# Attention heads' small products in other slots of a hand-planned decoder block, and ALiBi slopes moved into two scales

## The chip, the cores and the metric

One NeuronCore of a Trainium2 chip runs the whole program. The metric is the device time of one execution in microseconds; it was 438.44 us, the median of three runs (438.3 to 439.01). TensorE (PE) multiplies matrices, VectorE (DVE), ScalarE (ACT) and GpSimd (POOL) work on elements, SyncE (SP) issues most transfers. Each engine executes its instructions in the order in which the program writes them.

## The reference

One decoder block on 256 tokens of width 1024 in float32. With n = rmsnorm(x):

```
cu, cg, q, k, v, gc, ga = split(n @ w_in)
y_conv = silu(layernorm(causal_conv31(cu * sigmoid(cg)) + dw_b)) @ w_conv_out
att    = per head: softmax(rms(q) rms(k)^T / sqrt(128) - slope_h * distance, causal) @ v
merged = sigmoid(gc) * y_conv + sigmoid(ga) * (att @ w_attn_out)
h      = x + merged @ w_out
out    = h + (silu(r @ w_gate) * (r @ w_up)) @ w_down,   r = rmsnorm(h)
```

There are 8 heads of width 128, and slope_h = 2^-(h+1). All 256 tokens lie in one attention block, so no past block is selected and the attention is an ordinary causal one with a linear bias.

## The kernel before

**Main stream.** The weights come in pieces of 512 KB, one for each *slot*. For each piece ScalarE rounds it to a high part `whi` (line 154), VectorE (or GpSimd for some odd pieces between 12 and 60) subtracts it for the low part `wlo` (line 155), both six slots ahead of their use, and PE makes products in three terms, high by high, high by low, low by high (`mm3`, lines 173 to 175). A slot of the first 80 has 12 products of 512 columns, six for tokens 0 to 127 and six for tokens 128 to 255. The order of the slots is fixed: convolution inputs 0 to 15; q, k, v of heads 0 to 3 in 16 to 27; q, k, v of heads 4 to 7 in 28 to 39; gates 40 to 55; attention output (`ao`) 56 to 63; convolution output (`co`) 64 to 71; `wo` 72 to 79; then gate and up (`gu`), then down (`dn`).

**Small work beside it.** The rest is put into slots by four lists: `pre[slot]` stands ahead of the slot's first six products, `jobs[slot]` between the first six and the last six, `post[slot]` behind the last six, `late[slot]` after these. `busy` counts jobs of a slot.

**A head** (`head`) turns its q and k into columns (`turn`, line 429, tile `tq`), multiplies them (`score`, lines 439 and 440, tile `sc`), adds distances that ScalarE has scaled by the head's slope (line 437) and takes the row's extreme on VectorE (`most`), exponentiates two slots later, divides one slot after that, transposes the probabilities four slots after the score (`turn_p`, line 465, tile `tp`) and multiplies them with the values one slot later (`values`, lines 473 and 474, tile `pv`). All of these write one of two PSUM banks of tag `tr`.

**The convolution** runs as 31 taps for each of 8 channel groups on VectorE (line 273), two groups ("channels" here) at a time. `refill` (line 261, tile `cv`) transposes the next two groups into PSUM. `norm_stats` (line 336, tile `ytr`) transposes the finished pair back, and after the last pair layernorm's scale is made and `norm_back` (line 359, tile `yb`) makes silu on ScalarE (line 363), its high part `yh` (line 365) and its low part `yl` (line 366), the operands of `co`.

**The planner.** `run_taps` puts taps behind a slot as long as an estimated sum of VectorE's work, `load["dve"]`, stays below that of PE's, `load["pe"]`, plus 1.0. Each slot adds 2.6 (`SLOT`) to PE's sum and 1.14 (`LOW_PART`) to VectorE's unless GpSimd makes the low part; a tap adds 0.4 (0.53 when one channel alone is left); `pe_side` and `dve_side` add what small work costs in its slot; VectorE's sum is never below PE's less 2.6. So in which slot a tap, a refill, the statistics and `norm_back` stand follows from these sums. A pair's refill comes two slots after its predecessor's end, its statistics three or more, and `norm_back` two and three slots after the last statistics.

Of the kernel before, what the change touches and what calls it, by code (L numbers as in the profile page):

```python
# [9 lines left out]
F32 = mybir.dt.float32  # L10
F32R = mybir.dt.float32r
BF16 = mybir.dt.bfloat16
AF = mybir.ActivationFunctionType
# [3 lines left out]
P = 128  # L17
# [3 lines left out]
H = 8  # L21
# [4 lines left out]
CW = 512  # L26
G = 2
EPS = 1e-6
U = G * CW // P
SHIFT = 48  # L30
BIG = 1e30
# [3 lines left out]
C_QG = 4 * KD  # L35
# [7 lines left out]
SPL_BUFS = 8  # L43
AHEAD = 6

HEAD_STEP = ((0, 3, 6, 9), (0, 3, 5, 7))

SLOT = 2.6
LOW_PART = 1.14
# [3 lines left out]
REFILL = 2  # L53
# [34 lines left out]
def hybrid_block(ctx: ExitStack, tc: tile.TileContext, x, xT, par, w_in, w_co, w_ao, w_o, w_gu, w_dn, out):  # L88
    nc = tc.nc

    cst = ctx.enter_context(tc.tile_pool(name="cst", bufs=1))
# [13 lines left out]
    pre, jobs, post, late = (defaultdict(list) for _ in range(4))  # L105
    busy = defaultdict(int)
# [128 lines left out]
    rstd = cst.tile([P, T], F32, name="rstd")  # L235
    rhalf = cst.tile([P, T], F32, name="rhalf")
    rstd2 = cst.tile([P, T], F32, name="rstd2")
    gqs = cst.tile([P, 1], F32, name="gqs")

    def r1(t):  # L240
        return rstd[:, t : t + 1]
# [15 lines left out]
    def refill(ch):  # L257

        j, cv = ch["next"], ch["cv"]
        for t in range(T):  # L260
            nc.tensor.transpose(cv[:, KC - 1 + t * P : KC - 1 + (t + 1) * P],
                                ca[j // 2][:, t, (j % 2) * P : (j % 2 + 1) * P], ident)
        cacc[j] = ea.tile([P, S], F32, tag="cacc", bufs=4, name=f"cacc{j}")
        ch["j"], ch["k"], ch["next"] = j, 0, j + 2
# [11 lines left out]
    def run_taps(slot, until):  # L276
        while load["dve"] + TAP <= until:
            live = [ch for ch in chains if ch["j"] is not None]
            if not live:
                return  # L280
            load["turn"] += 1
            ch = live[load["turn"] % len(live)]
            conv_tap(ch)
            load["dve"] += TAP if len(live) > 1 else TAP_ALONE
            if ch["k"] == KC:
                j, ch["j"] = ch["j"], None
                want_refill(slot, ch)
                if j % 2:
                    last = j == KD - 1
                    at_ = slot + 3  # L290
                    while not last and busy[at_] > 1:
                        at_ += 1
                    busy[at_] += 1
                    jobs[at_].append(lambda p=j // 2: norm_stats(p))
                    pe_side[at_] += 0.45
                    dve_side[at_] += 0.7
                    if last:
                        for i in range(4):
                            jobs[at_ + 2 + i // 2].append(lambda i=i: norm_back(2 * i))

    def want_refill(slot, ch):
        j = ch["next"]
        if j < KD and j // 2 in ca:
            clear(ch)
            slot += REFILL
            post[slot].append(lambda: refill(ch))
            pe_side[slot] += 0.25
            dve_side[slot] += 0.1

# [20 lines left out]
    def norm_stats(p):  # L330
        if not yt:
            yt[0] = ea.tile([P, T, D], F32, tag="yt", name="yt")
        tr = bank(f"ytr{p}", T, 256)
        for t in range(T):
            for j in range(2):
                nc.tensor.transpose(tr[:, t, j * P : (j + 1) * P], cacc[2 * p + j][:, t * P : (t + 1) * P], ident)
        nc.scalar.copy(yt[0][:, :, p * 256 : (p + 1) * 256], tr)
        for t in range(T):
            nc.vector.bn_stats(bst[:, t, p, :], tr[:, t, :])
        if p == KD // 2 - 1:  # L340
            norm_scale()
# [64 lines left out]
    def v_done(b):  # L406
        def done(slot, acc):
            def evac(t):
                if not vs:
                    vs[0] = ea.tile([P, T, D], F32, tag="vs", name="vs")  # L410
                nc.scalar.activation(vs[0][:, t, b * CW : (b + 1) * CW], acc[t], AF.Copy, scale=r1(t))

            late[slot + 1].append(lambda: evac(0))
            late[slot + 2].append(lambda: evac(1))
            for i in range(4):
                head(slot + 1 + i, slot + 2 + HEAD_STEP[b][i], 4 * b + i)
        return done

    def head(first, slot, h):
        hs = slice((h % 4) * P, (h % 4 + 1) * P)  # L420
        vh = slice(h * P, (h + 1) * P)
        halves = ((0, slice(0, 1)), (1, slice(1, 3)))
        s = {}

        def turn():
            tq = bank(f"tq{h}", 4, P)
            for i, n in enumerate("qk"):
                for t in range(T):
                    nc.tensor.transpose(tq[:, 2 * i + t, :], qk[n, h // 4][:, t, hs], ident)
            s["q"] = sm.tile([P, S], F32, tag="qT", bufs=4, name=f"qT{h}")  # L430
            s["k"] = sm.tile([P, S], F32, tag="kT", bufs=4, name=f"kT{h}")
            nc.scalar.activation(s["q"], tq[:, 0:2, :], AF.Copy, scale=gqs)
            nc.scalar.activation(s["k"], tq[:, 2:4, :], AF.Copy, scale=prm[:, C_KG : C_KG + 1])

        def score():
            s["bias"] = sm.tile([P, 3, P], F32, tag="bias", name=f"bias{h}")
            nc.scalar.mul(s["bias"], dist, 2.0 ** (-8.0 * (h + 1) / H))
            s["sc"] = bank(f"sc{h}", 4, P)
            nc.tensor.matmul(s["sc"][:, 1:3, :], s["q"][:, P:], s["k"], start=True, stop=True)
            nc.tensor.matmul(s["sc"][:, 0, :], s["q"][:, :P], s["k"][:, :P], start=True, stop=True)  # L440
            most()

        def most():
            s["nmx"] = sm.tile([P, T], F32, tag="nmx", name=f"nmx{h}")
            for t, b in halves:
                nc.vector.tensor_tensor_reduce(s["bias"][:, b, :], s["sc"][:, b, :], s["bias"][:, b, :], scale=-1.0,
                                               scalar=3.0e38, op0=ALU.add, op1=ALU.min,
                                               accum_out=s["nmx"][:, t : t + 1])

        def expo():  # L450
            p = s["p"] = sm.tile([P, 3, P], F32, tag="p", name=f"p{h}")
            den = s["den"] = sm.tile([P, T], F32, tag="den", name=f"den{h}")
            for t, b in halves:
                nc.scalar.activation(p[:, b, :], s["bias"][:, b, :], AF.Exp, bias=s["nmx"][:, t : t + 1], scale=-1.0,
                                     accum_out=den[:, t : t + 1])
            nc.gpsimd.tensor_tensor(den, den, mone, op=ALU.pow)

        def divide():
            for t, b in halves:
                nc.scalar.activation(s["p"][:, b, :], s["p"][:, b, :], AF.Copy, scale=s["den"][:, t : t + 1])  # L460

        def turn_p():
            tp = bank(f"tp{h}", 4, P)
            for i in range(3):
                nc.tensor.transpose(tp[:, i, :], s["p"][:, i, :], ident)
            s["pT"] = sm.tile([P, 3, P], F32, tag="pT", name=f"pT{h}")
            nc.scalar.copy(s["pT"], tp[:, 0:3, :])

        def values():
            if not aoT:  # L470
                aoT[0] = pair("ao")
            pv = bank(f"pv{h}", S)
            nc.tensor.matmul(pv, vs[0][:, 0, vh], s["pT"][:, 0:2, :], start=True, stop=False)
            nc.tensor.matmul(pv[:, P:], vs[0][:, 1, vh], s["pT"][:, 2, :], start=False, stop=True)
            nc.scalar.copy(aoT[0][0][:, h, :], pv)
            nc.vector.tensor_sub(aoT[0][1][:, h, :], pv, aoT[0][0][:, h, :].bitcast(F32))

        for i in (first, slot, slot + 4, slot + 5):
            busy[i] += 1
        pe_side[first] += 0.45  # L480
        pe_side[slot] += 0.65
        pe_side[slot + 4] += 0.35
        pe_side[slot + 5] += 0.65
        dve_side[slot] += 0.7
        dve_side[slot + 5] += 0.35
        jobs[first].append(turn)
        jobs[slot].append(score)
        pre[slot + 2].append(expo)
        pre[slot + 3].append(divide)
        jobs[slot + 4].append(turn_p)  # L490
        jobs[slot + 5].append(values)


    sgs = ea.tile([P, 2, T, D], F32, tag="sgs", name="sgs")
# [229 lines left out]
    def first_norm():  # L724
        ss = bank("ss", T)
        for t in range(T):
            nc.tensor.matmul(ss[:, t : t + 1], sq[:, 0, t * P : (t + 1) * P], ones, start=True, stop=True)
        nc.vector.tensor_scalar(rstd, ss, 1.0 / D, EPS, op0=ALU.mult, op1=ALU.add)
        nc.gpsimd.tensor_tensor(rstd, rstd, mhalf[:, :T], op=ALU.pow)
        nc.gpsimd.tensor_scalar_mul(rhalf, rstd, 0.5)  # L730
        nc.gpsimd.tensor_scalar_mul(gqs, prm[:, C_QG : C_QG + 1], float(P) ** -0.5)

    post[4].append(first_norm)
    late[0].append(lambda: nc.scalar.dma_start(prm, par))
# [108 lines left out]
```

## Time and profile before

| | |
|---|---|
| median of three runs | 438.44 us (438.3 to 439.01) |
| the profiled execution | 437.82 us, span 436.0 us |
| TensorE clock granted | 0.999 of full speed |
| PE busy | 431.2 us, 99% of the span |
| VectorE, ScalarE, GpSimd busy | 314.8, 248.1, 87.3 us (72, 57, 20%) |
| transfers | 80.30 MB, 184 GB/s on average |

The profile is of one execution. PE's busy time counts pipelined products with modelled ends, so the distances between their starts say more than the share. A slot can be found in the trace by counting 12 products of the main stream.

### The profile page before, as it was taken

To read this page: it belongs to the slowest core of one execution; us is meant where nothing else is said; L and a number is where in the kernel's file an instruction comes from. 1 tells how busy PE (TensorE), PEld (TensorE's weight loads), DVE (VectorE), ACT (ScalarE), POOL (GpSimd) and SP (SyncE) were. 2 spreads that over 40 slices of the span, in tenths; PEclk is the share of its full clock that TensorE was granted. 3 is DMA by queue.
4 is the path that set the end of the run, shared out by engine and by line. 5 is a ranking of instruction groups with operands and counts; after the bars stand their busy time and mean duration, and the time that the engine had idled before them with its cause. 6 is when DMAs were issued, how large, how long until landed. Compare 5 with 4: busy or idle time off the path is not lost.

```text
span 436.0 us, 6861 instructions
## 1 busy us (share of the span) xinstructions
PE 431.2 (99%) x2514; PEld 376.4 (86%) x2514; DVE 314.8 (72%) x558; ACT 248.1 (57%) x451; POOL 87.3 (20%) x74
## 2 busy tenths in 40 slices
PE   8999999999999999999999999999999999999997
PEld 5788888888888888888888899999999999888886
DVE  4989999898889799967678368666666666644501
ACT  6765456789998676639435276455444555533300
POOL 1624465644572534200000000000000000000000
PEclk9999999999999999999999999999999999999999
DMA  8986665355445444654936536555555555775001
GB/s 277 337 284 224 230 260 186 132 194 209 144 142 165 153 138 144 194 177 149 309 122 190 188 106 232 168 192 193 194 196 196 190 196 193 247 228 201 37 0 50
DMA packets 23202, 80.30 MB, mean 184 GB/s; under 512 B 2560, under 2 KB 2944, under 8 KB 23168
## 3 DMA queue, kind: packets, MB, share of 16 engines
q1 hardware_dynamic: 22752, 78.66, 53.5%
q10 hardware_dynamic: 416, 1.19, 0.8%
q8 instruction: 20, 0.33, 0.3%
q14 instruction: 14, 0.11, 0.1%
HBM read 78.80 MB, written 1.05 MB: 183 GB/s over the span
## 4 chain that ended last, share of the span: by engine, by line
PE 95%; ACT 1%; DMA 1%; DVE 1%; SPq 1%; issue 0%
PE gu L191 9%; PE gu L192 9%; PE gu L190 9%; PE dn L174 4%; PE dn L175 4%; PE dn L173 4%; PE g L175 3%; PE g L173 3%; PE g L174 3%; PE conv L175 3%; PE conv L173 3%; PE conv L174 3%; PE k L175 2%; PE k L173 2%; PE q L175 2%; PE v L175 2%
## 5 line engine op out<-in xcount | busy, mean ns | idle before, releaser
L154 ACT CAST whi<-raw 128x1024 fp32r<-128x1024 f32 (+1 forms) x149 | 150.9, 1033 | 40.2 <-PE dn L174 21.4
L155 DVE TENSOR_TENSOR wlo<-raw,whi 128x1024 fp32r<-128x1024 f32 (+1 forms) x125 | 153.4, 1245 | 25.3 <-ACT whi L154 24.5
L190 PE MATMUL gu<-hh,whi 128*128 128x256 f32 x352 | 97.6, 277 | 0.0
L191 PE MATMUL gu<-hl,whi 128*128 128x256 f32 x352 | 97.4, 277 | 0.1
L273 DVE SCALAR_TENSOR_TENSOR cacc<-cv,prm,cacc 128x256 f32<-128x256 f32 x240 | 97.1, 473 | 0.2
L192 PE MATMUL gu<-hh,wlo 128*128 128x256 f32 x352 | 97.2, 276 | 0.0
L155 POOL TENSOR_TENSOR wlo<-raw,whi 128x1024 fp32r<-128x1024 f32 x24 | 59.3, 2473 | 51.1 <-ACT whi L154 46.2
L191 PEld LDWEIGHTS gu<-hl,whi 128*128 128x128 f32 x352 | 66.1, 188 | 0.4 <-DVE hl L571 0.3
L190 PEld LDWEIGHTS gu<-hh,whi 128*128 128x128 f32 x352 | 66.1, 188 | 0.3 <-ACT hh L570 0.2
L192 PEld LDWEIGHTS gu<-hh,wlo 128*128 128x128 f32 x352 | 66.1, 188 | 0.0
L174 PE MATMUL dn<-whi,fl 128*128 128x512 f32 x82 | 31.9, 389 | 0.0
L173 PE MATMUL dn<-whi,fh 128*128 128x512 f32 x82 | 31.9, 389 | 0.0
L175 PE MATMUL dn<-wlo,fh 128*128 128x512 f32 x82 | 31.9, 389 | 0.0
L173 PE MATMUL g<-whi,xgh 128*128 128x512 f32 x64 | 26.3, 412 | 0.0
L173 PE MATMUL conv<-whi,xgh 128*128 128x512 f32 x64 | 25.7, 402 | 0.2 <-ACT whi L154 0.2
L626 DVE TENSOR_TENSOR f<-gu,fs 128x256 f32<-128x256 f32 x22 | 9.2, 423 | 23.1 <-PE gu L192 23.1
L175 PE MATMUL conv<-wlo,xgh 128*128 128x512 f32 x64 | 25.2, 394 | 0.4 <-DVE wlo L155 0.4
L175 PE MATMUL g<-wlo,xgh 128*128 128x512 f32 x64 | 25.1, 393 | 0.0
L174 PE MATMUL g<-whi,xgl 128*128 128x512 f32 x64 | 24.9, 390 | 0.0
L174 PE MATMUL conv<-whi,xgl 128*128 128x512 f32 x64 | 24.9, 390 | 0.0
L633 ACT CAST fh<-f 128x256 fp32r<-128x256 f32 x22 | 8.9, 406 | 26.8 <-DVE f L626 26.7
L622 ACT ACTIVATE fs<-fg 128x256 f32<-128x256 f32 x22 | 9.1, 417 | 25.4 <-DVE fg L618 25.4
(163 smaller groups left out, 744.7 us busy)
## 6 DMA issues: line engine op xcount, KB each, us to landing
raw<-in_w_in SPq DMA_DIRECT2D x53, 512.0 KB, 4.3
raw<-in_w_gu SPq DMA_DIRECT2D x44, 512.0 KB, 3.3
raw<-in_w_dn SPq DMA_DIRECT2D x22, 512.0 KB, 4.1
raw<-in_w_ao SPq DMA_DIRECT2D x8, 512.0 KB, 3.2
raw<-in_w_co SPq DMA_DIRECT2D x8, 512.0 KB, 3.3
raw<-in_w_o SPq DMA_DIRECT2D x8, 512.0 KB, 4.7
raw<-in_w_in SPq DMA_DIRECT2D x6, 256.0 KB, 5.1
xs<-in_x ACTq DMA_DIRECT2D x1, 1024.0 KB, 7.2
```

Source lines behind the costliest of these rows:

```text
L154: nc.scalar.copy(hi[i][:, part, :], r[:, part, :])
L155: eng.tensor_sub(lo[i][:, part, :], r[:, part, :], hi[i][:, part, :].bitcast(F32))
L173: nc.tensor.matmul(acc, xh[:, k, tok], hi[i][:, j, cols], start=(k == first), stop=False)
L174: nc.tensor.matmul(acc, xl[:, k, tok], hi[i][:, j, cols], start=False, stop=False)
L175: nc.tensor.matmul(acc, xh[:, k, tok], lo[i][:, j, cols], start=False, stop=(k == last))
L190: nc.tensor.matmul(acc, hi[i][:, u, :], xh[:, k, :], start=first, stop=False)
L191: nc.tensor.matmul(acc, hi[i][:, u, :], xl[:, k, :], start=False, stop=False)
L192: nc.tensor.matmul(acc, lo[i][:, u, :], xh[:, k, :], start=False, stop=last)
L273: nc.vector.scalar_tensor_tensor(cacc[j], src, w, cacc[j], op0=ALU.mult, op1=ALU.add)
L622: nc.scalar.activation(st["s"], st["g"], AF.Silu)
L626: nc.vector.tensor_mul(st["f"], acc, st["s"])
L633: nc.scalar.copy(ff[0][0][:, j, :], st["f"])
```

## The change

Six edits go together. (1) `values` of a head moves to the slot of the next head's `turn_p`; a group's last head keeps one slot after. (2) Heads 4 to 7 take the same distances as heads 0 to 3 (0, 3, 6, 9 slots instead of 0, 3, 5, 7), and their query turns the slots 1, 2, 4, 5 after the group's start. (3) `score` goes to the front of its slot's jobs. (4) A refill joins a slot's jobs when there are any, and stays behind the products otherwise. (5) The statistics of a pair, other than the last, go behind the refill if its slot has no job. (6) The slope leaves the bias: the query's scale is divided by it (eight scales on GpSimd instead of one), the unscaled distances are read by `most`, the row's extreme is multiplied by the slope on VectorE, and the exponential takes the slope as its scale; ScalarE's scaling of the distances is gone.

```diff
+SLOPES = [2.0 ** (-8.0 * (h + 1) / H) for h in range(H)]
-HEAD_STEP = ((0, 3, 6, 9), (0, 3, 5, 7))
+HEAD_STEP = (0, 3, 6, 9)
+HEAD_TURN = ((1, 2, 3, 4), (1, 2, 4, 5))
...
-    gqs = cst.tile([P, 1], F32, name="gqs")
+    gqs = cst.tile([P, H], F32, name="gqs")
...
                     at_ = slot + 3
+                    if not last and not busy[slot + REFILL]:
+                        at_ = slot + REFILL
                     while not last and busy[at_] > 1:
                         at_ += 1
-                    busy[at_] += 1
-                    jobs[at_].append(lambda p=j // 2: norm_stats(p))
+                    (post if at_ == slot + REFILL else jobs)[at_].append(lambda p=j // 2: norm_stats(p))
+                    busy[at_] += at_ != slot + REFILL
...
             slot += REFILL
-            post[slot].append(lambda: refill(ch))
+            (jobs if busy[slot] else post)[slot].append(lambda: refill(ch))
...
+            at_ = [slot + 2 + i for i in HEAD_STEP]
             for i in range(4):
-                head(slot + 1 + i, slot + 2 + HEAD_STEP[b][i], 4 * b + i)
+                head(slot + HEAD_TURN[b][i], at_[i], at_[i + 1] + 4 if i < 3 else at_[i] + 5, 4 * b + i)
...
-    def head(first, slot, h):
+    def head(first, slot, end, h):
...
-            nc.scalar.activation(s["q"], tq[:, 0:2, :], AF.Copy, scale=gqs)
+            nc.scalar.activation(s["q"], tq[:, 0:2, :], AF.Copy, scale=gqs[:, h : h + 1])
...
-            nc.scalar.mul(s["bias"], dist, 2.0 ** (-8.0 * (h + 1) / H))
...
-                nc.vector.tensor_tensor_reduce(s["bias"][:, b, :], s["sc"][:, b, :], s["bias"][:, b, :], scale=-1.0,
+                nc.vector.tensor_tensor_reduce(s["bias"][:, b, :], s["sc"][:, b, :], dist[:, b, :], scale=-1.0,
...
+            nc.vector.tensor_scalar_mul(s["nmx"], s["nmx"], SLOPES[h])
...
-                nc.scalar.activation(p[:, b, :], s["bias"][:, b, :], AF.Exp, bias=s["nmx"][:, t : t + 1], scale=-1.0,
+                nc.scalar.activation(p[:, b, :], s["bias"][:, b, :], AF.Exp, bias=s["nmx"][:, t : t + 1], scale=-SLOPES[h],
...
-        for i in (first, slot, slot + 4, slot + 5):
+        for i in (first, slot, slot + 4, end):
             busy[i] += 1
...
-        pe_side[slot + 5] += 0.65
+        pe_side[end] += 0.65
...
-        dve_side[slot + 5] += 0.35
+        dve_side[end] += 0.35
+        jobs[slot].insert(0, score)
         jobs[first].append(turn)
-        jobs[slot].append(score)
...
-        jobs[slot + 5].append(values)
+        jobs[end].append(values)
...
-        nc.gpsimd.tensor_scalar_mul(gqs, prm[:, C_QG : C_QG + 1], float(P) ** -0.5)
+        for h in range(H):
+            nc.gpsimd.tensor_scalar_mul(gqs[:, h : h + 1], prm[:, C_QG : C_QG + 1], float(P) ** -0.5 / SLOPES[h])
```

## Rows read from the trace of the kernel before

**Rows 1.** The page, part 1: busy us, share of the span and instructions by engine.

```profile
PE 431.2 (99%) x2514; PEld 376.4 (86%) x2514; DVE 314.8 (72%) x558; ACT 248.1 (57%) x451; POOL 87.3 (20%) x74
```

**Rows 2.** Waits of weight loads: waiter, releaser, total us, times, longest.

```profile
PEld gu L191 <- DVE hl L571: 0.3, 1, 0.3
...
PEld gu L190 <- ACT hh L570: 0.2, 1, 0.2
```

**Rows 3.** PE in order of time: start us, us, line, operation, out<-in, count.

```profile
102.93 0.40 PE L175 MATMUL k<-wlo,xgh 128*128 128x512 f32 x1
103.16 0.49 PE L465 MATMUL tp<-ident,p 128*128 128x128 f32 x3
...
103.73 0.39 PE L174 MATMUL k<-whi,xgl 128*128 128x512 f32 x1
...
104.89 0.60 PE L261 MATMUL cv<-ident,ca 128*128 128x128 f32 x4
...
195.63 0.39 PE L175 MATMUL ao<-wlo,aoh 128*128 128x512 f32 x1
195.86 1.04 PE L359 MATMUL yb<-ident,yt 128*128 128x128 f32 x8
...
196.97 0.40 PE L174 MATMUL ao<-whi,aol 128*128 128x512 f32 x1
...
198.11 0.39 PE L173 MATMUL ao<-whi,aoh 128*128 128x512 f32 x1
```

**Rows 4.** Groups by line and shape: count, busy us, mean ns of one.

```profile
L437 ACT ACTIVATE bias<-dist 128x384 f32<-128x384 f32 x8 | 4.4, 548 | 0.0
...
L731 POOL TENSOR_SCALAR gqs<-prm 128x1 f32<-128x1 f32 x1 | 0.2, 226 | 0.1
...
L728 DVE TENSOR_SCALAR rstd<-ss 128x2 f32<-128x2 f32 x1 | 0.1, 145 | 0.0
```

**Rows 5.** The chain in order of time (start, us, what): refills, last statistics.

```profile
105.05 0.44 PE cv L261 x4
...
147.28 0.44 PE cv L261 x4
...
190.12 0.44 PE ytr L336 x4
```

**Rows 6.** ScalarE in order of time, around the first transposes of `norm_back`.

```profile
196.50 1.02 ACT L363 ACTIVATE sl<-yb,prm 128x256 f32<-128x256 f32 x2 [3.43 <-PE yb L359]
197.56 0.62 ACT L365 CAST yh<-sl 128x512 fp32r<-128x512 f32 x1
```

**Rows 7.** VectorE in order of time: last taps, normalisation, a split, the low part.

```profile
183.49 1.26 DVE L273 SCALAR_TENSOR_TENSOR cacc<-cv,prm,cacc 128x256 f32<-128x256 f32 x3
...
193.37 1.54 DVE L348 TENSOR_SCALAR yt<-yt,mv,lr 128x1024 f32<-128x1024 f32 x2 [1.10 <-POOL lr L231]
...
195.96 1.28 DVE L512 SCALAR_TENSOR_TENSOR sgs<-sgs,ao 128x512 f32<-128x512 f32 x2
197.16 1.22 DVE L155 TENSOR_TENSOR wlo<-raw,whi 128x1024 fp32r<-128x1024 f32 x1
198.29 0.69 DVE L366 TENSOR_TENSOR yl<-sl,yh 128x512 fp32r<-128x512 f32 x1
```

**Rows 8.** All engines in order of time: a weight load that waits for a low part.

```profile
252.03 0.48 DVE L571 SCALAR_TENSOR_TENSOR hl<-htr,prm,hh 128x256 fp32r<-128x256 f32 x1 [0.54 <-ACT hh L570]
...
252.56 0.19 PEld L191 LDWEIGHTS gu<-hl,whi 128*128 128x128 f32 x1 [0.33 <-DVE hl L571]
252.57 0.39 PE L191 MATMUL gu<-hl,whi 128*128 128x256 f32 x1
...
252.79 0.28 PE L192 MATMUL gu<-hh,wlo 128*128 128x256 f32 x1
...
252.91 0.28 PE L190 MATMUL gu<-hh,whi 128*128 128x256 f32 x1
```

**Rows 9.** Stretch of eight transposes: us, busy by engine, granted clock, DMA.

```profile
195.80:196.70 0.90, 0.90 (x10) 0.83 (x8) 0.90 (x3) 0.20 (x1) 0.00 (x0) 1.00 0.00 0
```

## The prediction

> **What bounds the kernel now.** I read part 1 of the page first: TensorE (PE) is busy 431.2 of 436.0 us [rows 1]; its granted clock is 0.999 of full speed. Busy time of pipelined matmuls proves little, so the waits come second: after the first 20 us, weight loads wait for another engine in only two places, both at the start of the gate and up products, 0.3 and 0.2 us long [rows 2]. Third, the start times on PE. The main stream runs at one product each 0.228 us (five intervals from 196.97 to 198.11 [rows 3]), 12 to a slot, 2.72 us, and all that lengthens a slot is the small products in it. So PE issues without a break, and a time saved on another engine is worth nothing. Only two things count: how long the small products hold PE, and whether a wait appears on PE where there is none.
>
> **Fewer groups of small products.** What does an interruption cost? Three transposes of probabilities stretch the time from the product before them to the second after them from two intervals (0.456) to 103.73 − 102.93 = 0.80 us; eight transposes to 196.97 − 195.63 = 1.34 [rows 3]. The five more cost 0.54, so 0.108 each, and three 0.324: the interruption itself is 0.80 − 0.456 − 0.324 = 0.02 us. The next five intervals, from 103.73 to 104.89, take 1.16 where 1.14 is usual, another 0.02: at most 0.04 in all for a group that disappears. By the slots of heads and refills I count, over slots 21 to 55, 30 groups before and 25 after: values(h) joins turn_p(h+1) six times, a score stands beside a query turn three times instead of twice, but values with query turns, and score with values or probabilities, lose five pairings. Five fewer groups at 0 to 0.04 are 0 to 0.2 us; I take 0.1, the 0.02 of each that is sure. That is the whole gain on PE: the small products themselves stay the same 32 of the heads.
>
> **Slopes.** Eight scalings of the distances leave ScalarE (548 ns each, 4.4 us [rows 4]); PE waits for no ScalarE instruction there, so the gain is 0. In their place VectorE gets eight products of 128x2; the nearest row, a 128x2 VectorE operation, is 145 ns [rows 4], so 1.2 us, up to 2.2 if each costs twice that with the wait for the two minima. Behind each stand taps and weight splits that are made six slots ahead, and the transposes of the probabilities four slots later: a cover of more than a slot, so 0, and 0.15 to 0.3 each if it were gone. GpSimd gets eight scales of the query instead of one, 226 ns each [rows 4], 1.6 us more in slot 4, behind the reciprocal root that the gates want and before its first weight split, due three slots later: 0. The heads' later slots are harmless too: head 7's values go from slot 53 to 55, and are read as the attention output's eighth slice in slot 59.
>
> **What moves the convolution.** This is the part that decides. The moved terms enter the planner's running sums (2.6 a slot for PE, 1.14 for a split on VectorE, 0.4 a tap, taps allowed up to PE's sum plus 1.0), and these say in which slot a channel's 31st tap falls. I carried the sums through slot by slot from 0, both ways. For the kernel before they put the channel pairs' ends in slots 19, 31, 43 and 56, so refills in 21, 33, 45 and the last statistics in 59; the trace has the last two refills at 105.05 and 147.28 and the last statistics at 190.12 [rows 5], which are the slots 33, 45 and 59 when products are counted. With the change:
>
> Slot 21. The first norm_stats moves there from 22. PE's sum is 58.15 (57.70 + 0.45), VectorE's starts at 55.55 + 0.2 + 0.7 = 56.45, and 6 taps fit below 59.15, where 8 fitted (55.30 to 58.50 below 58.70). The pair's 62 taps fall 6, 4, 6, 4, 7, 3, 7, 4, 7, 5, 7, 2 to the slots from 21 on, so it ends in slot 32 (before 8, 3, 7, 3, 7, 3, 7, 5, 7, 5, 7, ending in 31).
> Slot 34. Slot 34 holds no head job any more, so refill and second statistics go behind its products; the taps restart one slot later than before. From 34 on: 3, 7, 5, 6, 4, 8, 4, 7, 5, 8, 4, 1. The pair's channels end in 44 and 45 (before 43), so the last two start in 46 and 47 (before 45).
> Slots 46 to 59. VectorE's sum starts at 136.65 − 2.60 = 134.05, and the taps fall 3, 6, 5, 6, 4, 8, 3, 7, 5, 4, 4, 3, 3, 1 (before, from 45 on: 8, 3, 6, 4, 7, 5, 7, 4, 8, 3, 4, 3). The odd channel has 30 taps at the end of slot 57 (171.06 + 0.4 is over 171.45, by 0.01: a narrow miss). It ends in 58, its neighbour in 59.
>
> So the last norm_stats falls in slot 58 + 3 = 61 (before 59), and norm_back's transposes in 63 and 64 (before 61 and 62). The convolution's output product still starts in slot 64, since the order of the stream is fixed, and needs slices 0 and 1 of yT at its first two products. The two spare slots are gone.
>
> **The price.** Take norm_back's first transpose as zero; before, it is 195.86. PE's six remaining products of the slot follow, and the next slot begins at 198.11, zero + 2.25 [rows 3]. ScalarE makes silu from 196.50 and the high part yh from 197.56 to 198.18, zero + 2.32 [rows 6]. VectorE makes the low part yl at 198.29 to 198.98, zero + 3.12 [rows 7]; there a weight split that began at 197.16 stood ahead of it, so without one it is zero + 3.04. A weight load started 0.05 after such a low part ended (252.03 + 0.48 to 252.56), and the product after the waiting one came 0.22 later, where 0.12 is usual [rows 8]. So in slot 64: the first product, on yh, starts at 2.38 instead of 2.25; the second, on yl, at about 3.1, and the third, with its load exposed, at 3.42 instead of 2.70. That is 0.7 us of PE standing still. Below, 0.0 if yT were ready; above, 1.9, if a weight split (1.23) stood ahead of yl once more. I take 0.7, since nothing of slot 64 is queued ahead of the low part, and the attention product's evacuation, which lay between the splits before, now runs in slots 60 and 64. The other slices (2, 3 in slot 65; 4 to 7 in 68) have over 1.5 us to spare.
>
> Sum: the profiled execution took 437.82 us (436.0 of span and 1.82 around it); 437.82 + 0.7 − 0.1 = 438.4. The median of the runs, 438.44, lies 0.6 above that execution, so the median to expect is 438.44 + 0.6 = 439.0. A change below 0.2%, 0.88 us, can't be told from none here; mine is 0.14%.
>
> [...]
>
> **Rivals.** (1) No wait: norm_back lands a slot earlier, or yT is ready. For it: the tap count at slot 57 misses by 0.01 only. Against: it is an exact sum, and it has all the slots of the trace right. Then only the merging counts: 438.44 − 0.1 = 438.3. This is also the case in which the change does what it says and it is worth nothing. Chance 0.20. (2) Slower: VectorE falls behind at the end of the convolution. Before, its normalisation was over at 193.37 + 1.54 = 194.91, 0.95 us ahead of the transposes that read it [rows 7]; the last tap was over at 184.75 (183.49 + 1.26), 5.4 us before the statistics read it (190.12) [rows 5, 7]. The last tap now stands two slots ahead of the statistics instead of three, so 2.7 us are left, and the attention product's evacuation (1.28 us) comes ahead of them. It decides if the normalisation ends more than 0.95 us later against PE's slots; a split and the evacuation late together, 2.5 us, would put PE 1.5 us behind there, in addition to 0.7 − 0.1: 440.5; half of it 439.8. Chance 0.12. [...] (4) Faster by over 0.2%: all five interruptions at 0.04 and no wait are 0.2 us, so something unseen would have to give 0.7 more: 437.5. Chance 0.05.
>
> **Numbers.** The forecast has 0.62, with its own range 438.6 to 439.6 (wait of 0.3 to 1.2 us); about a fifth of that, 0.12, is over the bound of 0.88 us. Slower: 0.12 + 0.12 + 0.01 = 0.25. Faster 0.05. Same 0.70. The range takes in rival 1 with the scatter of the runs (438.3 to 439.01), and half of rival 2: 437.9 to 440.1.
>
> **What would show it.** On PE: the last four ytr transposes 12 products a slot after slot 61 begins, eight yb transposes in the last attention product's slot and eight in the first slot of the co product; in the waits, two new rows of weight loads of co on yh (0.1) and yl (0.7). Groups: 25 in slots 21 to 55, and slots with values and probabilities about 1.03 us over 2.72. No wait on PE elsewhere than at the start and at gate and up. ScalarE busy 4.4 us less, VectorE about 1.2 more. The forecast is wrong if co's first slot is no longer than its products and transposes, if the last statistics stand in slot 59 or 60, or if PE waits at a refill, which would mean that VectorE is later than the sums say.

## The result and the profile after

The changed kernel takes 444.29 us (median of four runs, 443.55 to 445.41) against 438.41 us (438.3 to 439.01) for the kernel before on the same chip: ratio 1.0133, 95% interval 1.0110 to 1.0157. It is 5.9 us slower, where no measurable change had been forecast. The profiled execution took 444.21 us with a span of 442.4, which is 6.4 over the span before.

Part 1 of the page after (busy us, share, instructions), to be set beside [rows 1], and the engine line of its part 4, the chain that ended last:

```profile
PE 433.3 (98%) x2514; PEld 376.6 (85%) x2514; DVE 321.4 (73%) x566; ACT 245.3 (55%) x443; POOL 95.2 (22%) x81
...
PE 81%; DVE 10%; ACT 5%; POOL 1%; DMA 1%; issue 1%; SPq 1%; POOLq 0%; ACTq 0%
```

The number of PE's instructions is the same, 2514, and its busy time grew by 2.1 us only, so at least 4.3 of the 6.4 us are PE standing still (a product that follows a wait is itself shown longer, 0.50 us instead of 0.39 in rows further down). VectorE holds 10% of the chain; before it held 1%:

```profile
PE 95%; ACT 1%; DMA 1%; DVE 1%; SPq 1%; issue 0%
```

The waits view (waiter, releaser, total us, times, longest) names the places that [rows 2] did not have. Some of PE's own waits, of which the kernel before has none after the first 20 us:

```profile
PE tp L473 <- DVE nmx L453: 2.2, 3, 1.2
PE tq L437 <- DVE aol L484: 0.8, 1, 0.8
...
PE v L176 <- ACT q L401: 0.5, 1, 0.5
```

and some of those of its weight loads:

```profile
PEld co L177 <- DVE yl L371: 0.5, 1, 0.5
PEld co L176 <- DVE sgs L520: 0.5, 1, 0.5
...
PEld co L176 <- ACT yh L370: 0.4, 1, 0.4
PEld gu L194 <- DVE hl L579: 0.3, 1, 0.3
```

Only the last row, and a 0.2 us row of the same products on `hh`, have a counterpart in [rows 2].

To see where the 6.4 us are, I took the start of each slot's first main product and noted what the slot takes over 2.72 us, small products included. Sums in us, by stretches of slots, each from one profiled execution:

```
              6-20  21-27  28-35  36-47  48-55  56-63  64-67  68-79    sum
before        0.47   0.95   5.85   9.63   3.82   2.27   0.00   2.71   25.7
after         0.47   2.33   5.33  13.37   4.44   1.48   1.96   2.69   32.1
```

The difference is 6.4 us, the whole growth of the span. Part of each column is only moved work: slots 36 to 39 hold small products that slots 28 to 35 held before, and norm_back's second eight transposes went from slot 62 to 64. What isn't moved work are waits: 0.6 and 0.15 us in slots 23 and 24, 0.65 and 0.14 in 27 and 28, then 1.35, 0.9, 0.45 and 1.04 in 36, 39, 42 and 43, and 0.64, 0.29 and 0.15 in 64, 65 and 66: 6.4 together. Slots 0 to 5 have no part in this: summed the same way they are 2.52 us before and 2.45 after.

### The profile page after: what moved, and what is told of

It reads as the page before. It is cut to its first block, busy times and chain, and to the rows that moved or that the text cites. A ratio compares the mean times of both kernels' runs of the same rounds, so it can differ in the third digit from the quotient of the medians.

```text
span 442.4 us, 6852 instructions
## 1 busy us (share of the span) xinstructions
PE 433.3 (98%) x2514; PEld 376.6 (85%) x2514; DVE 321.4 (73%) x566; ACT 245.3 (55%) x443; POOL 95.2 (22%) x81
## 4 chain that ended last, share of the span: by engine, by line
PE 81%; DVE 10%; ACT 5%; POOL 1%; DMA 1%; issue 1%; SPq 1%; POOLq 0%; ACTq 0%
PE gu L194 9%; PE gu L195 9%; PE gu L193 9%; DVE cacc L276 5%; PE dn L178 4%; PE dn L176 4%; PE dn L177 4%; PE conv L178 3%; PE conv L176 3%; PE conv L177 3%; PE g L176 3%; PE g L178 3%; PE g L177 3%; DVE wlo L158 2%; PE q L176 2%; PE q L178 2%
## 5 line engine op out<-in xcount | busy, mean ns | idle before, releaser
L158 POOL TENSOR_TENSOR wlo<-raw,whi 128x1024 fp32r<-128x1024 f32 x24 | 61.6, 2572 | 43.1 <-ACT whi L157 38.4
L630 ACT ACTIVATE fs<-fg 128x256 f32<-128x256 f32 x22 | 9.1, 418 | 25.7 <-DVE fg L626 25.7
```

Source lines behind the costliest of these rows:

```text
L158: eng.tensor_sub(lo[i][:, part, :], r[:, part, :], hi[i][:, part, :].bitcast(F32))
L630: nc.scalar.activation(st["s"], st["g"], AF.Silu)
```

## The experiments

In what follows, "sum" is the entry that the kernel of the experiment would have in the last column of the table above, and each ratio is to the kernel before, with its 95% interval. Two accounts stand against each other in the expectations: theory Q, that VectorE's and ScalarE's queues run late, and rival W, that the pairing of one head's values with the next head's probabilities, through their two PSUM banks, costs the time.

**The slopes alone (on the kernel before).** Edit, beside the scales of the query and of the exponential:

```diff
-            nc.scalar.mul(s["bias"], dist, 2.0 ** (-8.0 * (h + 1) / H))
...
-                nc.vector.tensor_tensor_reduce(s["bias"][:, b, :], s["sc"][:, b, :], s["bias"][:, b, :], scale=-1.0,
+                nc.vector.tensor_tensor_reduce(s["bias"][:, b, :], s["sc"][:, b, :], dist[:, b, :], scale=-1.0,
...
+            nc.vector.tensor_scalar_mul(s["nmx"], s["nmx"], SLOPES[h])
```

> The kernel before with the slopes alone moved (query scale, exponential's scale, the 128x2 product on VectorE), its slots as they were. Theory Q (late queues: the 128x2 product is held while GpSimd makes a weight split): products of up to 1.9 us again wherever a split runs beside them, about half of the eight, but the banks of before leave a slot of room, so PE waits for at most 0.5 us: 438.4 to 438.9. Rival W (only the pairing of values with the next probabilities, through the two banks, costs time): products of about 0.17 us and 438.4. A time above 440 would put most of the loss on the slopes.

Measured: 439.14 against 438.32, ratio 1.0026 [1.0003, 1.0049], a little above theory Q's range. The small product takes 1162 ns in the mean, and PE waits 0.83 us in slots 40 to 42. So this part alone costs something, where 0 had been forecast. The profiled run lost another 1.1 us at the refill of slot 21, whose tile VectorE cleared late. The first small product runs at 94.7 us, long after, so this loss is not the product's. VectorE had been busy without a break since a weight split that took 3.37 us, 1.2 else, beside splits of GpSimd; that this split made it late is read off the trace, not tried. VectorE's split and GpSimd's two, in order of time (start, us):

```profile
53.42 3.37 DVE L156 TENSOR_TENSOR wlo<-raw,whi 128x1024 fp32r<-128x1024 f32 x1
```

```profile
53.29 5.76 POOL L156 TENSOR_TENSOR wlo<-raw,whi 128x1024 fp32r<-128x1024 f32 x2 [5.19 <-ACT whi L155]
```

**The product in two halves (on the kernel after).** The product's tile has two columns, one for each block of rows; here each column has an instruction of its own.

```diff
-            nc.vector.tensor_scalar_mul(s["nmx"], s["nmx"], SLOPES[h])
+            for t in range(T):
+                nc.vector.tensor_scalar_mul(s["nmx"][:, t : t + 1], s["nmx"][:, t : t + 1], SLOPES[h])
```

> The changed kernel with the 128x2 product done as two products of 128x1, all slots as in the change. Theory Q with the held product depending on its shape: the 128x1 products take about 0.15 us each and never over 0.3, slot 36 keeps its 1.35 us of waiting, slots 39, 42 and 43 (0.9, 0.45, 1.0) lose most of it: 442.0 to 443.0. If one-column products are held as well (any VectorE operation against any GpSimd operation): 444.2. Rival W: no change, 444.2.

Measured: 441.55, ratio 1.0079 [1.0053, 1.0105]; sum 29.0, 3.1 less than in the kernel after. The waits of slots 39, 42 and 43 are gone and 0.76 us stays in slot 36. That is theory Q's side, and 0.45 us below its range, because slot 36's wait fell too. Twice as many instructions, and the time falls. In the changed kernel the product stands so in VectorE's order of time:

```profile
116.01 0.28 DVE L453 CUSTOM_DVE_ANT_0 bias<-sc,dist 128x128 f32<-128x128 f32 x1
...
116.22 0.42 DVE L453 CUSTOM_DVE_ANT_0 bias<-sc,dist 128x256 f32<-128x256 f32 x1
...
116.68 1.67 DVE L456 TENSOR_SCALAR nmx<-nmx 128x2 f32<-128x2 f32 x1
...
127.45 1.90 DVE L456 TENSOR_SCALAR nmx<-nmx 128x2 f32<-128x2 f32 x1
```

and GpSimd did this meanwhile:

```profile
115.85 2.47 POOL L158 TENSOR_TENSOR wlo<-raw,whi 128x1024 fp32r<-128x1024 f32 x1 [1.52 <-ACT whi L157]
...
126.93 2.39 POOL L158 TENSOR_TENSOR wlo<-raw,whi 128x1024 fp32r<-128x1024 f32 x1
```

The reader is to add start and duration: the products end at 118.35 and 129.35, the splits at 118.32 and 129.32. Four of the eight products ran beside a split, and each lasted until that split was over (1.67 to 1.90 us); the other four took 0.17. The two reductions that stand ahead of the product, which read one operand from PSUM, ran beside the same split in 0.28 and 0.42 us, as elsewhere. The same product on one column was not held, as the next rows show. By line and shape (count, busy us, mean ns), the product after:

```profile
L456 DVE TENSOR_SCALAR nmx<-nmx 128x2 f32<-128x2 f32 x8 | 7.6, 952 | 0.3
```

and the one of a single column in this experiment:

```profile
L457 DVE TENSOR_SCALAR nmx<-nmx 128x1 f32<-128x1 f32 x16 | 2.2, 151 | 0.0
```

One pair of these in VectorE's order of time, and what GpSimd did then:

```profile
95.40 0.27 DVE L457 TENSOR_SCALAR nmx<-nmx 128x1 f32<-128x1 f32 x2
```

```profile
94.73 2.46 POOL L158 TENSOR_TENSOR wlo<-raw,whi 128x1024 fp32r<-128x1024 f32 x1 [2.99 <-ACT whi L157]
```

That pair ran inside GpSimd's split, which lasted to 97.19, and was not held. From 94 to 140 us three of the five pairs ran inside a split, and each of the five took 0.27 us.

**Values in their old slots (on the kernel after).**

```diff
-        jobs[end].append(values)
+        jobs[slot + 5].append(values)
```

> The changed kernel with values one slot after their own probabilities again (slot + 5), the planner's sums held as in the change so that taps, refills and statistics stand where they stood. Rival W: slots 36 to 43 lose their 3.7 us of waiting and nothing else changes: 440.5. Theory Q: the same or less, since a late VectorE also holds back the banks of score and query turns: 440.5 to 442. The waits at slots 23 to 28 (1.6 us) and 64 to 66 (1.1 us) stay in both.

Measured: 442.99, ratio 1.0110 [1.0088, 1.0132]; sum 30.4. The waits of transposes of probabilities go, but waits of query turns for VectorE's attention output grow to

```profile
PE tq L437 <- DVE aol L484: 1.5, 2, 0.8
```

and some 2.0 us still stand in slots 40, 41 and 44. Both theories missed, the time lying 1 us above the nearer range: with VectorE held by the product, moving the values only moves the wait.

**Statistics read a slot later (on the kernel after).** `norm_stats` in `post` keeps its transposes there; the instructions that read them (ScalarE's copy, VectorE's statistics) go to the head of the next slot.

```diff
-        nc.scalar.copy(yt[0][:, :, p * 256 : (p + 1) * 256], tr)
-        for t in range(T):
-            nc.vector.bn_stats(bst[:, t, p, :], tr[:, t, :])
+        def evac():
+            nc.scalar.copy(yt[0][:, :, p * 256 : (p + 1) * 256], tr)
+            for t in range(T):
+                nc.vector.bn_stats(bst[:, t, p, :], tr[:, t, :])
...
+            pre[then].append(evac)
```

> The changed kernel with the statistics' transposes where the change has them, but the ScalarE copy and VectorE statistics that read them one slot later in the queues, behind the squares of q and k. Theory Q: the waits at slots 23, 24, 27, 28 (1.6 us) go, and slot 36 (1.35 us), whose score stood behind a weight split that ScalarE made late, goes or halves: 441.3 to 442.5. Rival W: only 1.6 us go, slots 36 to 43 keep 3.7: 442.7.

Measured: 442.77, ratio 1.0104 [1.0078, 1.0130]; sum 30.0, 2.1 less. The time is the one that rival W gave, but the waits are theory Q's: all of slots 23 to 28 are gone, and slot 36's falls from 1.35 to 0.76. ScalarE's order of time in the changed kernel shows why:

```profile
68.55 0.59 ACT L342 COPY yt<-ytr 128x512 f32<-128x512 f32 x1 [4.57 <-PE ytr L341]
69.03 0.37 ACT L387 ACTIVATE junk<-q,rstd 128x128 f32<-128x128 f32 x1
...
73.46 2.18 ACT L401 ACTIVATE q<-q,m 128x128 f32<-128x128 f32 x8 [1.55 <-POOL m L394]
```

and here with the copy put back:

```profile
63.81 0.36 ACT L395 ACTIVATE junk<-q,rstd 128x128 f32<-128x128 f32 x1
...
68.49 0.59 ACT L345 COPY yt<-ytr 128x512 f32<-128x512 f32 x1 [2.76 <-PE ytr L342]
...
69.93 2.17 ACT L409 ACTIVATE q<-q,m 128x128 f32<-128x128 f32 x8
```

The copy stands ahead of the last four squares of q (`junk`) in ScalarE's queue and holds the engine idle for 4.57 us until PE has made the transposes. The squares come 5.2 us later than with the copy put back (69.03 against 63.81) and the scaling that frees q's accumulators 3.5 us (73.46 against 69.93), and the v product that takes those accumulators waits. On PE, after:

```profile
74.66 0.50 PE L176 MATMUL v<-whi,xgh 128*128 128x512 f32 x1 [0.47 <-ACT q L401]
```

**Both mended, and the slope in the reduction (on the kernel after).** The statistics as above, and no product at all: the reduction takes over its factor, and the exponential's scale is -1 again.

```diff
-                nc.vector.tensor_tensor_reduce(s["bias"][:, b, :], s["sc"][:, b, :], dist[:, b, :], scale=-1.0,
+                nc.vector.tensor_tensor_reduce(s["bias"][:, b, :], s["sc"][:, b, :], dist[:, b, :], scale=-SLOPES[h],
...
-            nc.vector.tensor_scalar_mul(s["nmx"], s["nmx"], SLOPES[h])
```

> The changed kernel without the 128x2 product (the slope goes into the scale of the instruction that takes the row's extreme, the exponential's scale is -1 again) and with the statistics' readers behind the squares. Theory Q: with both queues in time the pairing of values and probabilities costs nothing, so slots 23 to 43 have no wait and only the late convolution output is left (slots 64 to 66, 1.1 us): 439.0 to 439.6. Rival W: the pairing itself still costs in slots 36, 39, 42 and 43, at least 1 us of their 3.7: 440.3 or more.

Measured: 440.2, ratio 1.0042 [1.0030, 1.0053]; sum 27.5, between the two theories. What is left is 0.76 us in slot 36 and 1.06 in slots 64 to 66. On slot 36, VectorE's reading of the score of head 2 and PE's transposes of head 1's probabilities:

```profile
113.13 1.23 DVE L158 TENSOR_TENSOR wlo<-raw,whi 128x1024 fp32r<-128x1024 f32 x1 [0.18 <-ACT whi L157]
114.28 0.28 DVE L461 CUSTOM_DVE_ANT_0 bias<-sc,dist 128x128 f32<-128x128 f32 x1
...
114.48 0.42 DVE L461 CUSTOM_DVE_ANT_0 bias<-sc,dist 128x256 f32<-128x256 f32 x1
```

```profile
115.06 0.52 PE L480 MATMUL tp<-ident,p 128*128 128x128 f32 x3 [0.58 <-DVE nmx L461]
```

The small products, other than the refills, which have banks of their own, share two PSUM banks (line 104). Slot 35 holds a score, slot 36 now two groups, values of head 0 and then transposes for head 1; the second takes the bank of that score, which VectorE has not read yet. No data passes between the two: it is the bank that is waited for. Slots 39, 42, 48, 51 and 54 hold the same pair and wait for nothing (1.01 to 1.03 us over 2.72): there VectorE had read the score in time.

**Last statistics a slot earlier (on the one before).**

```diff
-                    at_ = slot + 3
+                    at_ = slot + (2 if last else 3)
```

> The kernel of the run above with the last statistics one slot earlier (60 instead of 61, so the convolution output's operands are made in 62 and 63). Theory Q, with the planner's sums as third cause: the waits of slots 64 to 66 go as well, no wait is left and five groups fewer remain: 438.2, level with the kernel before (438.3) or up to 0.2 us under it. If the last taps end too late for slot 60, PE waits there instead and the time stays at 439 or above.

Measured: 439.22, ratio 1.0022 [1.0013, 1.0030]; sum 26.7. Theory Q's 438.2 missed. No wait remains in slots 64 to 66; 0.76 us stays in slot 36, and 0.42 is new in slot 62, because the last statistics now stand in `post` and are read a slot later. The waits view has it as

```profile
PEld yb L372 <- DVE yt L361: 0.5, 1, 0.5
```

**Values in their old slots (on the one before).** The edit is that of the third experiment.

> The kernel of the run above with values in the slot after their own probabilities again, all else the same. It shows what the pairing is worth when nothing waits: by the kernel before's rows six pairings give 0 to 0.04 us each, so the slots' sum is 0.03 to 0.25 us longer here, and the time the same to within the scatter: 438.2 to 438.5. Rival W: 0.5 us or more shorter than the run above.

Measured: 438.74, ratio 1.0011 [1.0002, 1.0019]; sum 26.0, 0.67 less. That is rival W's side, and theory Q missed: the time is above its 438.5. Slot 36's wait is gone, and only slot 62's 0.42 is left.

**Last statistics read in their own slot (on the one before).**

```diff
-                    then = at_ + 1 if at_ == slot + REFILL else None
-                    (post if at_ == slot + REFILL else jobs)[at_].append(lambda p=j // 2, then=then: norm_stats(p, then))
+                    then = at_ + 1 if at_ == slot + REFILL and not last else None
+                    (post if then else jobs)[at_].append(lambda p=j // 2, then=then: norm_stats(p, then))
```

The last pair's statistics so stand between the slot's products, with their readers right behind them.

> The kernel b3 (no 128x2 product, statistics' readers behind the squares, values in their own slot) with the last statistics between the products of slot 60 instead of behind them, so that the normalisation is over before slot 62. By the account of three causes no wait of PE is left after the first 20 us: the 0.42 us that b3 still waits at the yb transposes in slot 62 go, and the slots from 21 on are 0.1 us shorter in sum than in the kernel before: 438.0 to 438.4, no difference that can be measured. If it is still 0.4 us or more above the kernel before, something beside the three causes costs time.

Measured: 438.19 against 438.03, ratio 1.0004 [0.9995, 1.0013]; sum 25.6. After the first 21 us weight loads wait nowhere but at gate and up, as in [rows 2]:

```profile
PEld gu L194 <- DVE hl L586: 0.3, 1, 0.3
PEld gu L193 <- ACT hh L585: 0.2, 1, 0.2
```

What is left of the change here (heads 4 to 7 moved, the pairings of scores and refills, the slopes) takes the slots 0.1 us below those of the kernel before, and that can't be told from none. It has 30 groups of small products in slots 21 to 55, as many as the kernel before.

**Slopes without the product (on the kernel before).** The first experiment's edit, with the reduction's scale in place of the product.

> The kernel before with the slopes moved but no 128x2 product (as in the two runs above). Theory Q: the 0.26% of the run with the product came from the product; without it slots 40 to 42 have no wait: 438.2 to 438.5, the same as before. If the eight query scales on GpSimd are what delays VectorE early on, slot 21 waits for a refill here too and the time is 439 or more.

Measured: 438.08, ratio 1.0000 [0.9989, 1.0011]; sum 25.7, as before. So neither the missing scalings on ScalarE nor GpSimd's eight scales cost or give anything that can be measured; the slopes' price is the product alone. No wait at slot 21 either, though the eight scales are there.

The steps from after to the last version add up: the product 3.1 (32.1 to 29.0), the copy ahead of the squares another 1.5 (to 27.5, with the halves folded away as well; on the kernel after alone it is 2.1, since both causes delay slot 36), the late statistics 0.8 and 0.4, the values beside the next head's probabilities 0.7: 6.5 us, and the slots stand at 25.6 where they stood at 25.7 before.

## Why the prediction was wrong

The forecast was 439.0, and 444.29 is outside its range. By its steps:

- **What bounds the kernel** held: PE issued without a break, so the waits made elsewhere, 6.4 us, came through whole. Two small slips change nothing: weight loads had a third wait after the first 20 us (0.2 us for `ss`, at 20.4), and twelve intervals of 0.228 us are 2.74, where slots without small products take 2.72.
- **Fewer groups** held in its sizes: 25 groups, and a slot with values and probabilities takes 1.01 to 1.03 us over 2.72, as forecast. What fewer groups give is shown by the versions with sums 26.7 and 26.0, which differ in values' slots alone and have 25 and 30 groups: without the 0.76 of slot 36 the 25 groups are 0.1 us shorter, the forecast value. (The 0.1 us by which the last version is below the kernel before is not this gain, since both have 30.) What the step left out is the bank that a second group in a slot has to wait for, 0.76 us in slot 36.
- **Slopes: this step failed.** It priced the product by a 128x2 operation of 145 ns [rows 4] and put it under a "cover of more than a slot, so 0". The product takes 952 ns in the mean, 7.6 us in all, because GpSimd's splits hold it (1.67 to 1.90 us beside one, 0.17 otherwise); VectorE's busy time grew by 6.6 us, not 1.2. (ScalarE's fell by 2.8 us where 4.4 had been forecast; why is open.) The row that priced it stands at 24.8 us, where GpSimd had no split; its input `ss` is also a PSUM bank, which the product's is not, and no run tells whether that counts. The fallback, 0.15 to 0.3 for each of eight, gives 1.2 to 2.4 us, still under the 3.1 that the product's halves took away. The cover was no slot at all where two small groups stand in one: those need VectorE to have freed their bank within the slot (slot 36 waited 1.35 us).
- **What moves the convolution** held to the slot: last transposes `ytr` in slot 61, `yb` in 63 and 64. The chain after, beside [rows 5]:

```profile
200.77 0.44 PE ytr L341 x4
...
206.68 0.45 PE yb L364 x4
```

But this step followed slots and not queues. Moving the first statistics from slot 22 to the end of slot 21 was costed as sums of the planner; that ScalarE's copy passes the squares of q in its queue, and stops them, was not looked at: 1.5 to 2.1 us.

- **The price at slot 64** was right in place and size: 0.7 forecast, 0.64 measured in slot 64 and 0.1 ahead of its first product. VectorE's low part and PE around it, after:

```profile
208.87 0.69 DVE L371 TENSOR_TENSOR yl<-sl,yh 128x512 fp32r<-128x512 f32 x1 [1.02 <-ACT yh L370]
```

```profile
208.88 0.51 PE L176 MATMUL co<-whi,yh 128*128 128x512 f32 x1
209.61 0.50 PE L177 MATMUL co<-whi,yl 128*128 128x512 f32 x1 [0.22 <-DVE yl L371]
```

For the slices in slots 65 to 68 no wait shows, as forecast, but slots 65 and 66 lose another 0.44: the accumulators of co's second half wait for VectorE to read the attention product's (the `sgs` row of the waits). The prediction had that reading in slot 64; it stands behind a low part that began at 214.80, and began at 215.40, in slot 65.

- **The rivals**: rival 2 had the right engine, VectorE, in the wrong place. VectorE was late in the heads' slots, 36 to 43, not at the convolution's end. "No wait on PE elsewhere than at the start and at gate and up" was the sentence that the waits view refuted. The 0.01 in the sum of chances for slower is for a lower TensorE clock, which no run shows: the mean granted clock was 0.996 or more in every run and 0.999 to 1.000 in the changed kernel's four. It was 1.00 over eight transposes in one group before [rows 9], and 1.00 after from 86 to 176 us, where the heads' groups stand.

Shown by experiment are the product, the copy's place, the pairing in slot 36 and the late statistics. That GpSimd's splits hold the product rests on the ends: all four 128x2 products that ran beside a split in the changed kernel ended 0.02 to 0.03 us after it, and the four others took 0.17 us. What makes a product last to the split's end was not shown; no run took GpSimd's splits away.

## What to carry to other kernels

Price a small VectorE instruction by the longest GpSimd instruction that can run beside it, unless a row shows the same shape beside one (here 0.17 us became 1.67 to 1.90 beside splits of 2.39 to 2.84); folding the factor into an instruction that is there already cost nothing here (ratio 1.0000). When a step is moved, list on each engine what its readers now stand ahead of: an early reader of a late result stops everything behind it (here ScalarE, for 4.57 us). Five groups fewer are worth 0.1 us on PE here, and two groups in one slot, with two banks between them, turn VectorE's slack of a slot into none: 0.76 us in the one place of six where it came late.

## What was not expected of the hardware

A 128x2 `tensor_scalar` on VectorE took 0.17 us in the changed kernel or, beside a GpSimd split, 1.67 to 1.90 us, ending 0.02 to 0.03 us after that split; the same operation on one column took 0.15 us in the mean, sixteen times, beside such splits too.

The splits themselves show the same in the kernel before. Each of the six that VectorE began while GpSimd was at its own ended 1.08 or 1.09 us after that one, and took 1.35 to 2.17 us instead of 1.2: the earlier it had begun, the longer. One pair, VectorE's and GpSimd's:

```profile
144.47 2.17 DVE L155 TENSOR_TENSOR wlo<-raw,whi 128x1024 fp32r<-128x1024 f32 x1 [0.30 <-ACT whi L154]
```

```profile
143.15 2.41 POOL L155 TENSOR_TENSOR wlo<-raw,whi 128x1024 fp32r<-128x1024 f32 x1 [5.07 <-ACT whi L154]
```

The first ends at 146.64, the second at 145.56. The 3.37 us split of the first experiment also began (53.42) while GpSimd was at its own (53.29). So the two do not slow each other down evenly: VectorE's, begun later, ended 1.08 us after the other, nearly the 1.2 us that it takes alone, while the other took its usual 2.40 to 2.42. The same shows on GpSimd: its 128x2 power of the denominators takes 0.88 us in the mean where it took 0.71 before, and the two long ones of eight, 1.17 and 1.58 us, began beside a split on VectorE and ended 0.6 us after it.
